# A gated linear attention core rebuilt: wide subtractions, products on VectorE, grouped state updates

## The chip, the cores and the metric

The kernel runs on one core of a Trainium2 chip. The metric is device time in microseconds (us) of one execution, from its launch to its end; lower is better. The median of three runs of the kernel before is 3993.8 us.

## The reference

The program is a backbone of two layers over 2048 latent rows and 256 context rows of 1024 channels, in float32. Layer one is latent attention; the change doesn't touch it. Layer two is bidirectional gated linear attention with 4 heads, 128 key channels and 256 value channels a head. What matters of it, for one direction:

```python
def step(s, inp):
    qc, kc, vc, gc = inp
    bc = jnp.cumsum(gc, axis=2)
    o_inter = jnp.einsum('bhcd,bhde->bhce', qc * jnp.exp(bc), s)
    diff = bc[:, :, :, None, :] - bc[:, :, None, :, :]
    decay = jnp.exp(jnp.where(causal[:, :, None], diff, -jnp.inf))
    a = jnp.einsum('bhid,bhijd->bhij', qc, kc[:, :, None, :, :] * decay)
    o = o_inter + jnp.einsum('bhij,bhje->bhie', a, vc)
    blast = bc[:, :, -1:, :]
    s_new = jnp.exp(blast[:, :, 0, :])[..., None] * s + jnp.einsum('bhcd,bhce->bhde', kc * jnp.exp(blast - bc), vc)
    return s_new, o
```

The outputs of both directions are added, normalised per head, multiplied by silu(gate), projected and added to the stream; a last norm follows.

## The kernel before, in words

Layer two works on chunks of 128 rows, and on blocks of four chunks (512 rows), with channels on the partitions for q, k and the running log decays b. Its input projections are in `fill` (a generator that yields after each small piece: six matmuls of `terms`, L894 to L896, in tile pp). One head's recurrence is in `core(h)`, a generator too.

The loops of a head: first a backward sweep over the context and the blocks 3, 2, 1, 0, which stores the backward state that each chunk reads (s_b); per block `stage1` loads b, k and v, scans the decays (L1026) and makes the decayed keys (`khat`, L1030: subtraction on VectorE, exponential on ScalarE, product on GpSimd), `khat_rows` transposes them (L1045) and copies them to kt_ (L1047), and `update` adds one chunk to the state (L1052, then L1056 on VectorE). Then the blocks 0 to 3 forward. Within a chunk the 128x128 scores are put together by seven levels: at level li the rows are paired in halves of 64 >> li, and each pair of halves meets at the border between them, so that all exponents stay sums of log decays. `factors` (L1091 on) makes one level's decayed q and k in the tile ex (two halves of 512 columns): four subtractions on VectorE (L1102), one exponential on ScalarE (L1103), one product with q and k on GpSimd (L1104). `pairs` multiplies keys by queries in quarters of 64x64 (`quarters`, L1113, tile pg) and puts them into the scores `at`: level 0 as plain copies (L1123, L1124), the others by masked copies (L1128), two per level. `middle` prepares a block (qe, the keys' factors, the diagonal). At the end of a block come the output products (L1197 to L1199, tile po) with a state update after each chunk, the norm, the gate (`gate`, `gate2`: three activations and a product on GpSimd, L1159) and a store.

Factors run two levels ahead of pairs. The order of the work: the program draws pieces of `fill` between the yields of `core`, in proportion to the yields' weights (L1225 on); the framework then sets each engine's order, which may differ a little from the program's:

```python
    NCORE, NFILL, LEAD = 114, 215, 20
    for h in range(3):
        i = 0
        for w in core(h):
            i += w or 1
            while done < NFILL * (h + min(i / NCORE, 1)) + LEAD:
                next(proj, None)
```

With the last head the projections run out; its blocks are then interleaved with the output projection of layer two (`out_all`, tile py).

Of the kernel before, what the change touches and what calls it, by code (L numbers as in the profile page):

```python
# [19 lines left out]
P = 128  # L20
# [4 lines left out]
KT = D // P  # L25
# [10 lines left out]
class K:  # L36
    """Helpers around one TileContext."""
# [17 lines left out]
    def mm3(self, ps, terms):  # L55
        """ps = sum of lhsT.T @ rhs over terms (aH, aL, bH, bL), each product in three exact parts."""
        nc = self.nc
        n = len(terms)
        for i, (ah, al, bh, bl) in enumerate(terms):
            nc.tensor.matmul(ps, ah, bh, start=(i == 0), stop=False)  # L60
            nc.tensor.matmul(ps, ah, bl, start=False, stop=False)  # L61
            nc.tensor.matmul(ps, al, bh, start=False, stop=(i == n - 1))  # L62


def modulation_block(k, layer, nb, w, wp, ps, pt, gT, shT, ng, I, sel, condT, gates, gbc_d, bufs, tag="mod_s", bias=None):
    """512 columns of silu(cond) @ ada_w + ada_b: to shT and gT (channels on the partitions), or as gate rows to DRAM.
    w: the KT row blocks of the weight. Four row blocks at a time, each on its quarter of the array's columns; sel sums."""
# [40 lines left out]
def rstd_col(k, pool, ss, n, mhalf):  # L108
    """(ss / n + eps) ** -0.5 on a column."""
# [8 lines left out]
def body(ctx, tc, I, out, stop=99, dbg=None):  # L118
# [84 lines left out]
    with pool("p1", 2) as sp, pool("ps1", 2, space=PSUM) as psp:  # L203
# [11 lines left out]
        # the columns of shift and scale wait where the gate's weights go later  # L215
# [29 lines left out]
        def kv_weights():  # L245
            """mla_w_ukv in two parts, where the latents' columns were; behind it, the first chunk's kv latents."""
# [174 lines left out]
    def load_k(pr, ci):  # L421
        """One chunk of a pair's keys; what it returns puts it in place, in two parts."""
# [29 lines left out]
    def fetch(limit=2):  # L452
        """The next operands' load, and the parts of those that a former call loaded."""
# [6 lines left out]
    def maxima():  # L460
        """One piece per yield: the maxima of the scores' leading part go to row 96 of the queries."""
# [109 lines left out]
    with pool("p3", 2) as sp, pool("ps3", 2, space=PSUM) as psp:  # L571
# [65 lines left out]
        def mods():  # L637
            """The conditioning that later phases need, in small pieces."""
# [8 lines left out]
        def first_o():  # L647
            """The first rows' attention output, in two parts."""
# [7 lines left out]
        def first_y(oh, ol):  # L656
            """Their output projection, while the last sums are on their way."""
# [11 lines left out]
        def out_load(b):  # L669
            """w_out's rows 512 b and on."""  # L670
# [8 lines left out]
        def out_weights(b, raw):  # L679
            """They go in two parts where the keys were."""  # L680
# [64 lines left out]
    # one head's columns of the GLA input projection, in two parts: [q | gate] (0) or [k | v] (1)  # L745
# [16 lines left out]
    masks = wg.tile([P, 7, P], mybir.dt.uint8, name="masks")  # L762
    reset = wg.tile([P, 512], BF16, name="reset")
    gbias = wg.tile([P, 2, 4], F32, name="gbias")
    def prep_all(sp):
# [3 lines left out]
        for l0, l1 in ((0, 4), (4, 7)):  # L769
            ws = sp.tile([P, 512], F32, name="wsg", tag="wsg", bufs=4)  # L770
            nc.sync.dma_start(ws[:, :P * (l1 - l0)], I["masks"][:, l0:l1, :].rearrange("p l t -> p (l t)"))
            nc.vector.tensor_copy(masks[:, l0:l1, :].rearrange("p l t -> p (l t)"), ws[:, :P * (l1 - l0)])
# [117 lines left out]
    def terms(ps, ts):  # L890
        """ps = the sum over ts, an even share of it per yield."""
# [31 lines left out]
    def keys(h, ci, hk, g):  # L923
        """Columns of q (0) or k (1) of one chunk."""
# [27 lines left out]
    def rows(h, ci, hk, g):  # L952
        """Columns of gate (0) or v (1) of one chunk, rows on the partitions."""
# [14 lines left out]
    def next_h():  # L968
        """The next chunk of h; the one after it is on its way."""
# [6 lines left out]
    def fill():  # L976
        """All projections, a small piece per yield: a head's k, v and decays come with q and gate of the head before."""
# [31 lines left out]

    def block(h, blk, dirs, need_q):  # L1010
# [431 lines left out]
```

## Time and profile before

| what | value |
|---|---|
| runs | 3994.26, 3993.80, 3982.38 us |
| median | 3993.8 us |
| profiled execution, span from first to last instruction | 3977.7 us |
| instructions | 52504 |
| DMA | 451.70 MB, 114 GB/s |

The profile is of one execution; its span is the only time given for it, and it doesn't hold what lies before the first and after the last instruction. PE is TensorE, DVE VectorE, ACT ScalarE, POOL GpSimd. A row of a group of instructions gives line, engine, operation, tiles (written <- read), partitions x elements, count, then busy us and mean ns of one, then the idle time of the engine before them and what ended it. The ends of matmuls are modelled, so a busy PE isn't PE at its peak. TensorE's granted clock is given as a share of 2.4 GHz.

### The profile page before, as it was taken

The page shows a single profiled execution, that of the slowest core. Times are in us where ns is not written, and L with a number is a line of the kernel's source. Part 1 is how long each engine was busy: PE and PEld are TensorE (multiplying, and loading weights), DVE is VectorE, ACT ScalarE, POOL GpSimd, SP SyncE. Part 2 cuts the span into 40 slices and gives each one's busy share as a digit, 9 for nine tenths or more (in the row PEclk, how much of TensorE's full clock was granted, in tenths as well). Part 3 has the DMA queues.
Part 4 walks back from the last instruction along what each step waited for, and adds up shares of the span by engine and source line. Part 5 has one row for each costly group of instructions (what it writes and reads, how often), then busy time and mean ns, then how long its engine had stood idle before and what let it go on. Part 6 is the DMA issues. An engine that isn't in the chain of part 4 may idle for free.

```text
span 3977.7 us, 52504 instructions
## 1 busy us (share of the span) xinstructions
PE 3758.0 (94%) x20446; PEld 2748.3 (69%) x20446; DVE 2527.1 (64%) x3565; ACT 1345.2 (34%) x1879; POOL 1575.1 (40%) x899
## 2 busy tenths in 40 slices
PE   7999999999999999999999999999988889888798
PEld 5777887555555555555555555879977878877577
DVE  4433337777776777777777764652577686776863
ACT  2322222333333333333333433322243333433331
POOL 3121133646354534435363434650344343442430
PEclk9999999999999999999999999999999999999899
DMA  6211564111120201111010101877745546447332
GB/s 219 82 61 45 199 220 142 59 35 49 45 67 34 69 19 57 46 42 49 18 44 15 44 11 62 252 223 247 248 150 188 204 149 224 161 165 249 125 127 96
DMA packets 277393, 451.70 MB, mean 114 GB/s; under 512 B 21892, under 2 KB 178116, under 8 KB 265112
## 3 DMA queue, kind: packets, MB, share of 16 engines
q1 hardware_dynamic: 212648, 371.32, 28.3%
q10 hardware_dynamic: 64496, 77.02, 5.5%
q8 instruction: 161, 2.64, 0.3%
q14 instruction: 88, 0.72, 0.1%
HBM read 307.37 MB, written 140.71 MB: 113 GB/s over the span
## 4 chain that ended last, share of the span: by engine, by line
PE 71%; DVE 12%; issue 7%; DMA 4%; POOL 3%; ACT 1%; SPq 1%; POOLq 0%; ACTq 0%; DVEq 0%
PE st L594 20%; PE po L616 13%; PE pmx L475 8%; DVE ex L1102 5%; PE pj L61 4%; PE pj L60 4%; PE pj L62 4%; PE pp L894 2%; PE pp L896 2%; PE pp L895 2%; POOL ex L1104 1%; PE py L62 1%; PE py L60 1%; PE py L61 1%; DVE at L1128 1%
## 5 line engine op out<-in xcount | busy, mean ns | idle before, releaser
L476 DVE TENSOR_REDUCE mx<-pmx 128x1 f32<-128x512 f32 (+1 forms) x1312 | 762.9, 625 | 317.5 <-PE pmx L475 317.0
L596 ACT ACTIVATE pe<-st 128x1024 f32<-128x1024 f32 (+1 forms) x592 | 599.4, 1013 | 1004.9 <-PE st L594 979.0
L603 POOL TENSOR_TENSOR acc<-acc,pe 128x1024 f32<-128x1024 f32 x192 | 467.9, 2437 | 576.7 <-ACT pe L596 576.3
L616 PE MATMUL po<-pe,vt 128*64 128x512 f32 (+1 forms) x2368 | 572.4, 599 | 0.0
L603 DVE TENSOR_TENSOR acc<-acc,pe 128x1024 f32<-128x1024 f32 x256 | 439.4, 1716 | 96.6 <-ACT pe L596 96.6
L1104 POOL TENSOR_TENSOR ex<-ex,qk 128x1024 f32<-128x1024 f32 x112 | 286.4, 2563 | 285.6 <-ACT ex L1103 279.7
L594 PE MATMUL st<-qs,kb0h 97*128 97x512 f32 (+3 forms) x1184 | 375.4, 396 | 0.1
L594 PE MATMUL st<-qs,kb1h 97*128 97x512 f32 (+3 forms) x1184 | 374.9, 397 | 0.0
L616 PEld LDWEIGHTS po<-pe,vt 128*64 128x64 f32 x2368 | 156.9, 137 | 301.1 <-issue 297.8
L894 PE MATMUL pp<-w,ht 128*128 128x256 f32 x1088 | 334.3, 307 | 0.0
L1102 DVE TENSOR_TENSOR ex<-b 128x256 f32<-128x256 f32 x448 | 300.0, 724 | 16.2 <-PE pg L1113 9.8
L896 PE MATMUL pp<-w,ht 128*128 128x256 f32 x1088 | 309.8, 285 | 0.0
L895 PE MATMUL pp<-w,ht 128*128 128x256 f32 x1088 | 309.6, 285 | 0.0
L594 PEld LDWEIGHTS st<-qs,kb1h 97*128 97x128 f32 (+1 forms) x1184 | 218.3, 190 | 57.9 <-issue 12.2
L594 PEld LDWEIGHTS st<-qs,kb0h 97*128 97x128 f32 (+1 forms) x1184 | 219.9, 191 | 48.9 <-issue 4.2
L594 PE MATMUL st<-qs,kb1l 96*128 96x512 f32 (+1 forms) x592 | 232.3, 392 | 0.0
L594 PE MATMUL st<-qs,kb0l 96*128 96x512 f32 (+1 forms) x592 | 232.3, 392 | 0.0
L894 PE MATMUL pp<-ht,w 128*128 128x256 f32 (+1 forms) x616 | 191.5, 311 | 39.9 <-ACT vge L959 37.9
L1103 ACT ACTIVATE ex<-ex 128x1024 f32<-128x1024 f32 x112 | 118.7, 1060 | 291.7 <-DVE ex L1102 281.8
L475 PE MATMUL pmx<-kb0h,qs 96*128 96x512 f32 (+1 forms) x656 | 208.7, 397 | 8.7 <-DVE mx L476 5.6
L894 PEld LDWEIGHTS pp<-w,ht 128*128 128x128 f32 x1088 | 208.2, 191 | 6.5 <-DVE gm L944 0.2
L895 PEld LDWEIGHTS pp<-w,ht 128*128 128x128 f32 x1088 | 209.4, 192 | 2.5
(393 smaller groups left out, 7487.6 us busy)
## 6 DMA issues: line engine op xcount, KB each, us to landing
ht<-hh_d SPq DMA_DIRECT2D x44, 1024.0 KB
ht<-hl_d SPq DMA_DIRECT2D x44, 1024.0 KB
xt<-in_x SPq DMA_DIRECT2D x32, 512.0 KB
mod_w<-in_ada_w SPq DMA_DIRECT2D x16, 1024.0 KB
v<-gv_d SPq DMA_DIRECT2D x32, 512.0 KB
wsg<-in_gla_w_in SPq DMA_DIRECT2D x66, 192.0 KB
v_d<-vs ACTq DMA_DIRECT2D x18, 512.0 KB
vt<-v_d SPq DMA_DIRECT2D x8, 1152.0 KB
```

The costliest lines, as they stand in the source:

```text
L60: nc.tensor.matmul(ps, ah, bh, start=(i == 0), stop=False)
L475: nc.tensor.matmul(ps[:, :w], qs[0:96, 0, j, t * P:t * P + P], kh[0:96, j, b * 512:b * 512 + w], start=True, stop=True)
L476: nc.vector.reduce_max(mx[:, j * nq + t, b:b + 1], ps[:, :w], axis=AX.X)
L594: nc.tensor.matmul(st[:, j, :n], a, b, start=(i == 0), stop=(i == 2))
L596: nc.scalar.activation(pe[:, :, :n], st[:, :, :n], AF.Exp, scale=SCALE)
L603: eng.tensor_tensor(acc[:, :, :n], acc[:, :, :n], pe[:, :, :n], op=ALU.add)
L616: nc.tensor.matmul(po[64 * j:64 * j + 64, :n], vt[:, kt, 64 * j:64 * j + 64], pe[:, j, :n], start=(kt == 0), stop=(kt == nk - 1))
L894: nc.tensor.matmul(ps, ah, bh, start=(i == 0), stop=False)
L895: nc.tensor.matmul(ps, ah, bl, start=False, stop=False)
L896: nc.tensor.matmul(ps, al, bh, start=False, stop=(i == n - 1))
L1102: nc.vector.tensor_tensor(out_, a_, b_, op=ALU.subtract)
L1104: nc.gpsimd.tensor_tensor(ex, ex, c["qk"], op=ALU.mult)
```

## The change

The four subtractions of a level become one over both directions with all 1024 columns, from the decays at the border to a tile df; two exponentials with scale +1/16 and -1/16 read the right halves of df into ex. The last level, of single rows, decays q alone. The products of q and k (ex), of the state's keys (ke) and of the gate (gt) move from GpSimd to VectorE. The quarters lie side by side in pg (256 columns), and the masked copies go to a compact tile `ad` of 128x256, one per level, which two ScalarE copies place in `at` at the block's end. The state's matmuls of a block are issued together (`updates`), and VectorE's state steps (`advance`) follow. Yields are fewer and carry weights, with a sum of 148 a head. Buffers of df, ke, kt_, at and ad are single. The mask array is 7x64 columns instead of 7x128.

```diff
     def khat(d, qk, b, nch):
...
-        nc.gpsimd.tensor_tensor(e[:, :w], e[:, :w], qk[:, 1, :w], op=ALU.mult)
+        nc.vector.tensor_tensor(e[:, :w], e[:, :w], qk[:, 1, :w], op=ALU.mult)
...
-    def update(khat_c, v_c, tot_c, s_in, s_out):
-        ps = psp.tile([P, 512], F32, name="pk", tag="pk")
-        nc.tensor.matmul(ps[:, :256], khat_c, v_c, start=True, stop=True)
+    def updates(kh, v, chunks):
+        out_ = {}
+        for i, c in enumerate(chunks):
+            if i % 2 == 0:
+                ps = psp.tile([P, 2, 256], F32, name="pk", tag="pk")
+            nc.tensor.matmul(ps[:, i % 2, :], kh[:, c * P:c * P + P], v[:, c, :], start=True, stop=True)
+            out_[c] = ps[:, i % 2, :]
+        return out_
+    def advance(add, tot_c, s_in, s_out):
...
-            nc.vector.scalar_tensor_tensor(s_out, s_in, tot_c, ps[:, :256], op0=ALU.mult, op1=ALU.add)
+            nc.vector.scalar_tensor_tensor(s_out, s_in, tot_c, add, op0=ALU.mult, op1=ALU.add)
...
         def factors(c, li):
...
-            for out_, a_, b_ in ((ev[:, 0, :, 1, :], bv[:, 0, :, 1, :], r0), (ev[:, 0, :, 0, :], bv[:, 1, :, 0, :], r1),
-                                 (ev[:, 1, :, 0, :], r0, bv[:, 0, :, 0, :]), (ev[:, 1, :, 1, :], r1, bv[:, 1, :, 1, :])):
-                nc.vector.tensor_tensor(out_, a_, b_, op=ALU.subtract)
-            nc.scalar.activation(ex, ex, AF.Exp, scale=LOG)
-            nc.gpsimd.tensor_tensor(ex, ex, c["qk"], op=ALU.mult)
-            return ex
+            b = c["b"]
+            if hl == 1:
+                nc.vector.tensor_tensor(view(ex, 0, ((1, 2), (2, 256))), view(b, 512, ((-511, 2), (2, 256))), view(b, 513, ((-513, 2), (2, 256))), op=ALU.subtract)
+                nc.scalar.activation(ex[:, 0, :], ex[:, 0, :], AF.Exp, scale=LOG)
+                nc.vector.tensor_tensor(ex[:, 0, :], ex[:, 0, :], c["qk"][:, 0, :], op=ALU.mult)
+                return ex[:, 0, :], c["qk"][:, 1, :]
+            df = sp.tile([P, 2, 512], F32, name="df", tag="df", bufs=1)
+            nc.vector.tensor_tensor(view(df, 0, ((512, 2), (2 * hl, nn), (1, 2 * hl))), view(b, 0, ((512, 2), (2 * hl, nn), (1, 2 * hl))),
+                                    view(b, hl - 1, ((513, 2), (2 * hl, nn), (0, 2 * hl))), op=ALU.subtract)
+            for i, (o0, s0, sg) in enumerate(((512, hl - 512, LOG), (0, 512 + hl, -LOG))):
+                nc.scalar.activation(view(ex, 512 * i, ((hl, 2), (2 * hl, nn), (1, hl))), view(df, o0, ((s0, 2), (2 * hl, nn), (1, hl))), AF.Exp, scale=sg)
+            nc.vector.tensor_tensor(ex, ex, c["qk"], op=ALU.mult)
+            return ex[:, 0, :], ex[:, 1, :]
...
-            for u in range(2):
-                us = slice(64 * u, 64 * u + 64)
-                nc.vector.copy_predicated(half(c["at"], u, False), masks[us, li, us].unsqueeze(1).to_broadcast([64, 4, 64]), half(pg, u, False))
+            else:
+                nc.vector.copy_predicated(four(c["ad"]), masks[:, li, :].unsqueeze(1).to_broadcast([P, 4, 64]), four(pg))
+        def placed(c):
+            for u in range(2):
+                nc.scalar.copy(half(c["at"], u, False), four(c["ad"], slice(64 * u, 64 * u + 64)))
...
         def gate2(c):
-            sg = sp.tile([P, 4, 256], F32, name="sg", tag="ex", bufs=3)
+            sg = sp.tile([P, 4, 256], F32, name="sg", tag="df", bufs=1)
...
-            nc.gpsimd.tensor_tensor(c["gt"], c["gt"], sg, op=ALU.mult)
+            nc.vector.tensor_tensor(c["gt"], c["gt"], sg, op=ALU.mult)
...
                 pairs(c, li, exs[li])
-                yield 2
+                if li % 2 == 0:
+                    yield 5 if li in (2, 4) else 3
             c["kh"] = khat_rows(c["ke"], 4)
+            placed(c)
...
+            add = updates(c["kh"], c["v"], [i for i in range(4) if 4 * blk + i < 15])
+            ss = [s]
+            for i in range(4):
+                if i in add:
+                    s2 = sp.tile([P, 256], F32, name="sf", tag="sf", bufs=5)
+                    advance(add[i], c["tot"][:, 0, i:i + 1], ss[i], s2)
+                    ss.append(s2)
+            s = ss[-1]
+            yield 8 if cn else 2
...
-    NCORE, NFILL, LEAD = 114, 215, 20
+    NCORE, NFILL, LEAD = 148, 215, 20
...
-        while done < NFILL * 3 + LEAD + i * 1.2:
+        while done < NFILL * 3 + LEAD + i * 0.92:
...
-    for _ in main:
-        for _ in range(4):
+    for w in main:
+        for _ in range(round(2 * w)):
```

## Rows read from the trace of the kernel before

**Rows 1.** The page's first part: busy us (share of the span) x instructions.

```profile
PE 3758.0 (94%) x20446; PEld 2748.3 (69%) x20446; DVE 2527.1 (64%) x3565; ACT 1345.2 (34%) x1879; POOL 1575.1 (40%) x899
```

**Rows 2.** Busy time by stretch: length, busy us of each engine, TensorE's clock, DMA.

```profile
core 0: us, PE busy (x) PEld busy (x) DVE busy (x) ACT busy (x) POOL busy (x), PEclk, DMA share, GB/s
2820.00:3084.00 264.00, 230.07 (x2004) 215.47 (x2003) 189.11 (x298) 96.41 (x176) 111.92 (x62) 0.95 0.55 185
3084.00:3342.00 258.00, 223.31 (x1941) 207.75 (x1940) 189.23 (x299) 97.05 (x177) 109.41 (x62) 0.95 0.53 182
3342.00:3602.00 260.00, 227.49 (x1961) 210.74 (x1960) 185.88 (x294) 98.24 (x180) 104.55 (x54) 0.95 0.56 188
3602.00:3710.00 108.00, 79.39 (x626) 69.60 (x624) 82.75 (x121) 37.10 (x69) 37.81 (x18) 0.87 0.63 220
3710.00:3786.00 76.00, 61.49 (x349) 47.22 (x350) 59.08 (x89) 27.63 (x45) 29.74 (x15) 0.87 0.33 110
3786.00:3978.00 192.00, 177.80 (x967) 139.91 (x965) 96.07 (x161) 50.40 (x87) 38.38 (x27) 0.98 0.32 110
```

**Rows 3.** What TensorE waited for, 2850 to 3870: us in total, times, longest.

```profile
PE pg L1113 <- POOL ex L1104: 43.8, 34, 7.0
PE pp L894 <- ACT vge L959: 37.3, 9, 8.2
...
PE pk L1052 <- ACT kt__29738 L1047: 5.4, 1, 5.4
```

**Rows 4.** Who waited for whom, all engines, 2850 to 3870.

```profile
ACT ex L1103 <- DVE ex L1102: 281.8, 92, 7.3
POOL ex L1104 <- ACT ex L1103: 279.7, 90, 9.7
```

**Rows 5.** The timeline of two levels in head two: start us, us, engine, what.

```profile
3149.37 2.38 POOL L1104 TENSOR_TENSOR ex<-ex,qk 128x1024 f32<-128x1024 f32 x1 [3.91 <-ACT ex L1103]
...
3149.62 3.43 DVE L1102 TENSOR_TENSOR ex<-b 128x256 f32<-128x256 f32 x4
...
3153.14 1.06 ACT L1103 ACTIVATE ex<-ex 128x1024 f32<-128x1024 f32 x1 [3.85 <-DVE ex L1102]
...
3154.05 3.60 DVE L1102 TENSOR_TENSOR ex<-b 128x256 f32<-128x256 f32 x4
...
3154.28 2.42 POOL L1104 TENSOR_TENSOR ex<-ex,qk 128x1024 f32<-128x1024 f32 x1 [2.53 <-ACT ex L1103]
```

**Rows 6.** Durations of single lines: ns min/median/max, first and last start.

```profile
L1102 DVE TENSOR_TENSOR ex<-b x448: 402/418/2622, 2855.1 to 3866.0; 128x256 f32<-128x256 f32 x150
...
L1139 DVE TENSOR_TENSOR qe<-qe,qk x16: 1207/1227/2571, 2858.2 to 3780.1; 128x1024 f32<-128x1024 f32 x16
...
L1036 DVE TENSOR_TENSOR ke<-b x37: 418/680/2819, 2828.4 to 3740.2; 128x512 f32<-128x512 f32 x30, 128x256 f32<-128x256 f32 x7
...
L1037 ACT ACTIVATE ke<-ke x37: 408/632/640, 2829.1 to 3740.9; 128x512 f32<-128x512 f32 x30, 128x256 f32<-128x256 f32 x7
...
L1026 DVE TENSOR_TENSOR_SCAN b<-reset,b x53: 684/1225/3380, 2826.9 to 3739.1; 128x512 f32<-128x512 bf16 x46, 128x256 f32<-128x256 bf16 x7
```

**Rows 7.** VectorE's costliest groups in head two, 3084 to 3342.

```profile
L1102 DVE TENSOR_TENSOR ex<-b 128x256 f32<-128x256 f32 x112 | 75.9, 732 | 4.1 <-PE pg L1113 3.5
L1026 DVE TENSOR_TENSOR_SCAN b<-reset,b 128x512 f32<-128x512 bf16 (+1 forms) x14 | 22.2, 1594 | 8.8 <-DMA b<-ggf_d 4.7 <-DMA b<-ggb_d 4.1
L1128 DVE COPY_PREDICATED at<-masks,pg 64x256 f32<-64x256 uint8 x48 | 21.5, 448 | 2.5 <-PE pg L1113 1.2
```

**Rows 8.** VectorE's timeline in head two, 3133 to 3144.

```profile
3133.31 0.41 DVE L1054 COPY sf<-pk 128x256 f32<-128x256 f32 x1
...
3141.97 0.45 DVE L1128 COPY_PREDICATED at<-masks,pg 64x256 f32<-64x256 uint8 x1 [0.62 <-PE pg L1113]
3142.31 0.73 DVE L944 TENSOR_SCALAR gm<-pp,gbias 128x512 f32<-128x512 f32 x1
3143.08 0.46 DVE L1128 COPY_PREDICATED at<-masks,pg 64x256 f32<-64x256 uint8 x1
```

**Rows 9.** What VectorE waited for in head two, 3084 to 3342.

```profile
DVE s_b L1056 <- PE pk L1052: 11.7, 8, 2.6
DVE sf L1056 <- PE pk L1052: 10.8, 7, 2.5
```

More of the change, by code (lines that the diff above doesn't have):

```diff
@@ L768, in prep_all @@
             yield
[L769 to L772, printed above, removed]
+        ws = sp.tile([P, 512], F32, name="wsg", tag="wsg", bufs=4)
+        nc.sync.dma_start(ws[:, :7 * 64], I["masks"].rearrange("p l t -> p (l t)"))
+        nc.vector.tensor_copy(masks.rearrange("p l t -> p (l t)"), ws[:, :7 * 64])
         nc.vector.memset(reset, 1.0)
@@ L1008, in body, with view @@
     psp = cst.enter_context(pool("psc", 2, space=PSUM))
+    def view(t, off, dims):
+        a = t[:, 0, 0:1]
+        return bass.AP(tensor=a.tensor, offset=a.offset + off, ap=[list(a.ap[0])] + [list(d) for d in dims])
     def block(h, blk, dirs, need_q):
@@ L1072, in core @@
             kh = khat_rows(e, nch)
-            yield
+            yield 1
             if bi + 1 < len(order):
                 nxt = stage1(order[bi + 1])
-                yield
-            for i in range(nch - 1, -1, -1):
-                kc, vc, tc_ = kh[:, i * P:i * P + P], v[:, i, :], tot[:, 1, i:i + 1]
+                yield 2
+            chunks = [i for i in range(nch - 1, -1, -1) if blk < 0 or 4 * blk + i > 0]
+            add = updates(kh, v, chunks)
+            for i in chunks:
                 if blk < 0:
-                    update(kc, vc, tc_, None if i == 1 else sc, sc if i == 1 else s_b[:, 15, :])
-                elif 4 * blk + i > 0:
+                    advance(add[i], tot[:, 1, i:i + 1], None if i == 1 else sc, sc if i == 1 else s_b[:, 15, :])
+                else:
                     n = 4 * blk + i
-                    update(kc, vc, tc_, s_b[:, n, :], s_b[:, n - 1, :])
-                yield
-        s = None
-        qk, b, v, tot, nch = block(h, -1, (0,), False)
-        kh = khat_rows(khat(0, qk, b, nch), nch)
-        yield
+                    advance(add[i], tot[:, 1, i:i + 1], s_b[:, n, :], s_b[:, n - 1, :])
+            yield nch / 2
         def factors(c, li):
@@ L1158, in gate2 @@
             nc.scalar.activation(sg, sg, AF.Exp, scale=-1.0)
-            nc.gpsimd.tensor_tensor(c["gt"], c["gt"], sg, op=ALU.mult)
+            nc.vector.tensor_tensor(c["gt"], c["gt"], sg, op=ALU.mult)
+        qk, b, v, tot, nch = block(h, -1, (0,), False)
+        kh = khat_rows(khat(0, qk, b, nch), nch)
+        yield 1
         c = begin(0)
-        yield
+        yield 2
+        add = updates(kh, v, (0, 1))
+        s = None
         for i in range(2):
-            s2 = sp.tile([P, 256], F32, name="sf", tag="sf")
-            update(kh[:, i * P:i * P + P], v[:, i, :], tot[:, 0, i:i + 1], s, s2)
+            s2 = sp.tile([P, 256], F32, name="sf", tag="sf", bufs=5)
+            advance(add[i], tot[:, 0, i:i + 1], s, s2)
             s = s2
-            yield
+        yield 1
         middle(c)
         exs = [factors(c, 0), factors(c, 1)]
-        yield
+        yield 6
         for blk in range(4):
```

76 lines of the change are left out of this document (35 added, 41 removed).

## The prediction

> **What bounds the kernel now.** The page's first part comes first: TensorE is busy 3758.0 of 3977.7 us [rows 1]. That is an average over stages, so the stages follow. From 2820 us on the recurrence of layer two is woven into its projections. The stretches of the first three heads (264, 258 and 260 us, cut where a head's last block leaves) show TensorE busy 230.07, 223.31 and 227.49 us at a granted clock of 0.95, the start of the fourth head 79.39 of 108 us and 61.49 of 76 us at 0.87 [rows 2]. Idle time in these five is 33.9 + 34.7 + 32.5 + 28.6 + 14.5 = 144 us. A clock of 0.95 is a tenth of the time at 1.2 GHz instead of 2.4 GHz, after stretches in which TensorE waited; a tenth of 258 us at half speed is worth up to 13 us a head. So a head has at most 34.7 + 13 = 48 us to give, and its TensorE work is about 210 us. The last stretch, from 3786 us on, is busy 177.80 of 192 us [rows 2]: there TensorE is the bound.
>
> What it waits for stands in the waits: 43.8 us for the product ex on GpSimd (L1104), 37.3 us for the ScalarE copy vge that empties a projection's PSUM bank, and waits of up to 5.4 us for kt_, ScalarE's copy of the transposed keys [rows 3]; the kt_ wait occurs nine times, 25.6 us together. Behind these is a chain: ScalarE's exponential waits 281.8 us for VectorE's subtractions, GpSimd's product 279.7 us for that exponential [rows 4]. vge stands behind those exponentials on ScalarE. The timeline of two levels shows why the chain is slow [rows 5]: at 3149.62 VectorE starts four subtractions and ends them after 3.43 us, while GpSimd's product of the level before runs from 3149.37 for 2.38 us; at 3154.05 the same again, 3.60 us. A level takes 3154.05 - 3149.62 = 4.4 us there, and 4.9 us from product to product; I take 4.5. One subtraction alone takes 0.402 to 0.418 us, but the slowest 2.622, about a product longer [rows 6], and the mean in head two is 0.732 [rows 7]. So the two engines take turns, and the level costs their sum.
>
> **The change part by part, for one block of 512 rows.** A head is four blocks and a backward sweep. Head two (3084 to 3342) spends some 49 us on the sweep, up to the first sf copy at 3133.31 [rows 8], and 209 on four blocks: 52.3 each; TensorE's share of the 48 us is some 8.5 a block, the most a block can win.
>
> *Subtraction and product.* Four subtractions become one of 1024 elements. Nearest row: qe (L1139), a 128x1024 operation of two SBUF operands, one broadcast, 1.227 us median [rows 6]. The product on VectorE has the same shape: 1.227. The masked copy goes from two of 64x256 (mean 0.448 [rows 7]) to one of 128x256; same columns, 0.45. VectorE's work in a wide level is then 1.23 + 1.23 + 0.45 = 2.9 us, and the last level has half the elements: 0.68 + 0.68 + 0.45 = 1.8, with 0.68 from ke (L1036, 512 elements [rows 6]).
>
> *The new wait.* The product now stands on VectorE behind the subtraction and needs the exponentials between: two of 512 elements, 0.632 each by ke's exponential (L1037 [rows 6]), 1.26 us. The buffer df is single, so the next subtraction can't go ahead of them either. Whatever is queued behind the product (masked copies, state advances, VectorE's copies out of projection banks) waits too. Bounds of a wide level: 2.9 if all of this is filled, 2.9 + 1.26 = 4.15 if none. I take the middle, 3.5: the order on VectorE isn't the program's, a projection's gm stands between two masked copies of one level [rows 8], so part of the gap will be filled, but VectorE's ready work there is thin. Levels of a block: before 7 x 4.5 = 31.5; after 6 x 3.5 + 1.8 + 0.6 = 23.4. **Gain 8.1.** Bounds: 6 x 2.9 + 1.8 = 19.2 gives 12.3, 6 x 4.15 + 2.4 = 27.3 gives 4.2.
>
> *Work that comes to VectorE besides.* The keys' product (0.68) and the gate's product (1.23) leave GpSimd, with waits behind one exponential (0.63) and behind three of 1.06 us [rows 5]. Surely 1.9 us a block, at worst 1.9 + 0.63 + 3.2 = 5.7. Scans lose their turns with GpSimd: 1.594 mean against 1.225 median [rows 6, 7], two a block, 0.7 back. I take 2.5 net, nearer the low end, as the gate's loads and exponentials come two levels ahead of its use. **Net gain 8.1 - 2.5 = 5.6 a block**, under the 8.5. Twelve blocks of three heads: **67 us**.
>
> *State updates in groups.* VectorE waits in head two 11.7 and 10.8 us for single updates from TensorE [rows 9]; TensorE waits for kt_ as above. With all update matmuls together, more projection pieces stand between the transposes and the first update (3 x 215/148 = 4.4 instead of 2 x 215/114 = 3.8 in the sweep), and output matmuls no longer alternate with VectorE's state. Ends: nothing, and the 25.6 us of kt_. Two thirds of that lies in forward blocks, where the cap already counts it. I take **8 us**.
>
> *Fourth head.* From 3602 to 3786 projections run out and TensorE idles 43 us [rows 2], so the block's chain shows in full: two blocks x 5.6, and its kt_ wait of 5.4 [rows 3]: **17 us**. Its last two blocks lie under the output projection; nothing, since TensorE covers them; without that cover they would cost or give 5.6 each.
>
> *At nothing.* The masks' load and conversion become one each, before the first head, under projections. Fewer buffers (ke, kt_, at): each waits for transposes or products that precede it in program order; at worst 37 keys x the 1 us of a short wait, hidden while VectorE has other work. One exponential more per level, one scaling less and two placing copies more a block on ScalarE: about 2 us a block on an engine busy under half the time. New weights at the yields (148 for 114) keep 215 pieces of projection a head; a block gets 31 x 215/148 = 45 instead of 36, the sweep fewer. The levels keep 16/31 of a block's pieces instead of 14/19, which follows the shorter levels. On GpSimd the weight splits and the power of orr are freed of the queue.
>
> Sum: 67 + 8 + 17 = 92 us. The page gives the profiled execution's span, 3977.7 us, 16.1 under the median of the three runs, which also holds what lies around the span; nothing around it changes. 3993.8 - 92 = **3902 us**.
>
> **Rivals.** *VectorE becomes the bound.* For it: in head two its busy time barely falls. 112 subtractions (75.9 us) and 48 masked copies (21.5) go [rows 7]; 24 x 1.23 + 4 x 0.68 = 32 come for subtractions, 32 for products, 11 for masked copies, 6 for keys, 5 for the gate: 189 [rows 2] becomes 178, less 5 for scans. If every wait is exposed a block gains 4.2 - 5.0 = -0.8. Against it: order is free [rows 8]. Twelve blocks lose 10, the state groups give 8: about 3995 us. The Trainium skill, page "TensorE: Matmul & The Clock Gate", section Part 1, says of the architecture that VectorE's queue is strictly first in, first out. By that rule a product whose exponential is late holds all that was queued behind it, and the time would be this rival's unless the order was chosen well beforehand; the trace agrees in that VectorE sat idle for single updates [rows 9]. Chance 0.11.
>
> *The strided exponential is dear, and the kernel gets slower.* No row shows ScalarE reading and writing runs of 2 to 64 elements. If such an exponential costs twice the contiguous one, 1.26 us, a wide level is 2.9 + 2.5 = 5.4 us, 0.9 over today: 6 x 0.9 + 2.5 = 8 us a block lost, 14 blocks, 112 us: 4106. It decides from (4.5 - 2.9)/2 = 0.8 us each with nothing filled in. Against it: VectorE's subtractions have the same runs and stay at 0.418 [rows 6]. Chance 0.09.
>
> *The waits vanish.* TensorE is kept fed: 12 x 8.5 + 15 + 40 = 157 us: 3837. For it: 2.9 us a level. Chance 0.12. The forecast, from a quarter to all of the waits filled short of that, has 0.68.
>
> **The numbers.** The range 3835 to 3970 holds the forecast's bounds and the floor; it leaves out the slow rival and most of the first. 0.3% is 12 us, about what a measurement of this kernel can tell. Faster: 0.68 + 0.12 + half of 0.11; same: the rest of that; slower: 0.09.
>
> **What would show it.** Right: the wide subtraction and the product near 1.23 us; ScalarE's strided exponentials near 0.63; levels 3.5 us apart; TensorE's idle time in a head under 20 us and the clock near 1; GpSimd a few us a head. Wrong: blocks still 52 us apart with VectorE waiting for ex from ScalarE; exponentials over 0.8 us; the idle time moved to pp after vge, because ScalarE's copies now stand behind exponentials that wait for a later subtraction; po waiting for at behind the placing copies.

## The result and the profile after

| | before | after |
|---|---|---|
| median of 4 runs each, in turn on one chip | 3989.18 us (3982.38 to 3994.26) | 3832.68 us (3830.01 to 3834.88) |
| ratio, 95% interval | | 0.9623 [0.9597, 0.9648] |
| span of the profiled execution | 3977.7 us | 3828.1 us |

The kernel is 156 us faster, 150 in the profiled spans. The forecast was 92 us. The measured median lies 2.3 us under the low end of its range; the kernel before came out 4.6 us lower in this timing than the 3993.8 that the forecast starts from, and the ratio gives 0.9623 x 3993.8 = 3843 us, inside the range near that end. The time is about that of the rival "the waits vanish" (3837). The whole page first, as [rows 1]: GpSimd lost 380 us of busy time, VectorE 121, TensorE 55 at the same number of matmuls.

```profile
PE 3702.5 (97%) x20446; PEld 2717.6 (71%) x20446; DVE 2406.3 (63%) x3300; ACT 1356.5 (35%) x1991; POOL 1194.7 (31%) x731
```

The same six stretches as [rows 2], cut where a head's last block or the fourth head's first two leave (columns as there):

```profile
2820.00:3055.00 235.00, 224.38 (x2032) 213.46 (x2031) 157.84 (x229) 99.73 (x206) 13.85 (x20) 0.97 0.62 208
3055.00:3274.00 219.00, 210.35 (x1952) 199.17 (x1951) 160.01 (x236) 99.43 (x205) 13.91 (x20) 1.00 0.65 215
3274.00:3490.00 216.00, 209.48 (x1945) 198.23 (x1944) 160.03 (x232) 102.50 (x211) 8.40 (x12) 1.00 0.70 235
3490.00:3578.00 88.00, 69.79 (x605) 63.90 (x603) 71.87 (x99) 39.09 (x77) 1.85 (x1) 0.92 0.73 258
3578.00:3641.00 63.00, 56.95 (x348) 45.35 (x350) 48.61 (x66) 25.95 (x51) 2.67 (x4) 0.89 0.37 126
3641.00:3828.00 187.00, 176.12 (x986) 140.40 (x980) 89.52 (x134) 52.51 (x99) 9.81 (x15) 0.99 0.32 113
```

The stretches got 29, 39, 44, 20, 13 and 5 us shorter: 150, so the whole gain lies here. In head two TensorE's idle time went from 34.7 to 8.65 us, which is 26 of its 39; the other 13 are busy time (223.31 to 210.35 for 1941 and 1952 matmuls), with the granted clock up from 0.95 to 1.00. Over the first three heads the idle time fell by 75 us (101.1 to 25.8), the busy time by 37; over the fourth by 22 and 16.

Head two once more, cut between its backward sweep and its blocks, before and then after (columns as in [rows 2]):

```profile
3084.00:3133.00 49.00, 45.32 (x349) 43.78 (x348) 28.33 (x49) 17.30 (x33) 14.84 (x9) 1.00 0.74 257
3133.00:3342.00 209.00, 178.00 (x1594) 163.97 (x1593) 160.90 (x252) 79.75 (x144) 94.56 (x54) 0.94 0.49 164
```

```profile
3055.00:3093.00 38.00, 36.09 (x268) 33.94 (x266) 29.69 (x48) 15.79 (x33) 0.00 (x0) 1.00 0.87 295
3093.00:3274.00 181.00, 174.27 (x1686) 165.23 (x1685) 130.33 (x189) 83.64 (x172) 13.91 (x20) 1.00 0.60 198
```

Before, the sweep was nearly full (TensorE idle 3.7 of 49 us) and the blocks were not (31 of 209). After, some 80 to 90 matmuls have moved from the sweep into the blocks, and the blocks are shorter all the same. In every head, from the single records (a sweep runs from the end of the head before, in head one from 2820, to VectorE's first copy sf; the blocks from there to VectorE's last scaling of osb):

| head | sweep before | after | blocks before | after |
|---|---|---|---|---|
| one | 50.7 | 34.7 | 213.3 | 200.7 |
| two | 49.3 | 37.5 | 209.1 | 181.1 |
| three | 52.3 | 38.6 | 207.3 | 177.9 |
| four | 45.4 | 32.4 | 266.0 | 240.4 |

Of the 112 us of heads one to three, 42 lie in the sweeps and 70 in the twelve blocks; of the fourth head's 38, 13 lie in its sweep.

What TensorE waited for (2850 to 3720), beside [rows 3]:

```profile
PE pg L1131 <- DVE at L1141: 12.2, 2, 10.5
PE pp L893 <- ACT vge L958: 9.4, 6, 4.0
PE pg L1131 <- DVE ex L1118: 8.3, 5, 3.7
```

And the two waits of a level's chain, from the waits of all engines, beside [rows 4]:

```profile
ACT ex L1117 <- DVE df L1114: 132.9, 64, 6.2
...
DVE ex L1118 <- ACT ex L1117: 28.1, 41, 1.4
```

The wait for the product ex fell from 43.8 us to 8.3, that for vge from 37.3 to 9.4. VectorE stood still before its product for 28.1 us in all: 96 wide levels with two exponentials of 0.631 us each could have cost 121. How it is filled shows in VectorE's and ScalarE's timeline of two levels in head two:

```profile
3105.93 1.21 DVE L1114 TENSOR_TENSOR df<-b 128x1024 f32<-128x1024 f32 x1
3107.06 1.00 DVE L1143 COPY_PREDICATED ad<-masks,pg 128x256 f32<-128x256 uint8 x2
3107.25 1.15 ACT L1117 ACTIVATE ex<-df 128x512 f32<-128x512 f32 x2 [4.88 <-DVE df L1114]
3108.44 1.23 DVE L1118 TENSOR_TENSOR ex<-ex,qk 128x1024 f32<-128x1024 f32 x1 [0.38 <-ACT ex L1117]
3109.58 1.22 DVE L1114 TENSOR_TENSOR df<-b 128x1024 f32<-128x1024 f32 x1
...
3112.14 1.23 DVE L1118 TENSOR_TENSOR ex<-ex,qk 128x1024 f32<-128x1024 f32 x1 [1.34 <-ACT ex L1117]
```

Two masked copies of earlier levels stand in the first gap; the second level finds nothing and waits 1.34 us. From the start of the subtraction to the end of the product the first level takes 3109.67 - 3105.93 = 3.74 us. Before, it took 3156.70 - 3149.62 = 7.08 [rows 5].

VectorE's groups in head two beside [rows 7], and ScalarE's exponential there:

```profile
L1114 DVE TENSOR_TENSOR df<-b 128x1024 f32<-128x1024 f32 x24 | 29.4, 1227 | 0.0
L1118 DVE TENSOR_TENSOR ex<-ex,qk 128x1024 f32<-128x1024 f32 x24 | 29.2, 1219 | 5.7 <-ACT ex L1117 5.5
L1030 DVE TENSOR_TENSOR_SCAN b<-reset,b 128x512 f32<-128x512 bf16 (+1 forms) x14 | 16.0, 1142 | 3.6 <-DMA b<-ggb_d 3.6
L1143 DVE COPY_PREDICATED ad<-masks,pg 128x256 f32<-128x256 uint8 x24 | 10.7, 447 | 1.0 <-PE pg L1131 0.4
...
L1117 ACT ACTIVATE ex<-df 128x512 f32<-128x512 f32 x48 | 28.6, 631 | 35.4 <-DVE df L1114 35.4
```

**Delay, not pace.** From the single records of head two I took, for each level, the time from the start of its first subtraction to the end of its product:

| kernel | product on | levels | shortest / median / longest, us |
|---|---|---|---|
| before | GpSimd | 28 | 5.04 / 7.24 / 13.32 |
| after | VectorE | 24 wide | 3.66 / 4.26 / 16.57 |
| before, product moved (below) | VectorE | 28 | 3.78 / 5.38 / 11.19 |
| after, narrow subtractions (below) | VectorE | 28 | 3.78 / 4.92 / 9.47 |
| after, product moved back (below) | GpSimd | 24 wide | 5.00 / 7.18 / 21.73 |

The distance between levels changed far less. A block has two runs of wide levels, the first three ahead of the output products of the block before and the next three behind them. The gaps from one product's start to the next inside these runs, 48 in heads one to three, have a median of 4.6 us before and 4.3 after, a mean of 4.6 and 4.5. What became shorter in a block is the stretch between its two runs, from the third level's product to the fourth's (19.2 to 13.4 us, mean of 12), and from its last level to the next block's first (10.2 to 8.7, mean of 9).

### The profile page after: what moved, and what is told of

It reads as the page before. It is cut to its first block, busy times and chain, and to the rows that moved or that the text cites. A ratio compares the mean times of both kernels' runs of the same rounds, so it can differ in the third digit from the quotient of the medians.

```text
span 3828.1 us, 51918 instructions
## 1 busy us (share of the span) xinstructions
PE 3702.5 (97%) x20446; PEld 2717.6 (71%) x20446; DVE 2406.3 (63%) x3300; ACT 1356.5 (35%) x1991; POOL 1194.7 (31%) x731
## 4 chain that ended last, share of the span: by engine, by line
PE 76%; DMA 7%; DVE 6%; issue 6%; POOL 3%; ACT 2%; SPq 1%; POOLq 0%; ACTq 0%; DVEq 0%
PE st L594 20%; PE po L616 14%; PE pmx L475 8%; PE pj L61 5%; PE pj L60 5%; PE pj L62 5%; PE pp L893 2%; PE pp L894 2%; PE pp L895 2%; DMA wsg<-in_gla_w_in 2%; PE py L893 1%; PE py L895 1%; PE py L894 1%; PE pk L1060 1%; PE py L62 1%
## 5 line engine op out<-in xcount | busy, mean ns | idle before, releaser
L893 PE MATMUL pp<-w,ht 128*128 128x256 f32 x1088 | 317.9, 292 | 0.0
L894 PE MATMUL pp<-w,ht 128*128 128x256 f32 x1088 | 305.9, 281 | 0.0
L895 PE MATMUL pp<-w,ht 128*128 128x256 f32 x1088 | 304.9, 280 | 0.0
L1242 POOL TENSOR_TENSOR orr<-oss,mhalf 128x4 f32<-128x4 f32 x16 | 17.1, 1068 | 659.3 <-DVE oss L1241 659.3
L475 PE MATMUL pmx<-kb1h,qs 96*128 96x512 f32 (+1 forms) x656 | 205.0, 396 | 4.1 <-DVE mx L476 4.0
L893 PEld LDWEIGHTS pp<-w,ht 128*128 128x128 f32 x1088 | 205.8, 189 | 3.4
L894 PEld LDWEIGHTS pp<-w,ht 128*128 128x128 f32 x1088 | 205.9, 189 | 1.1
L895 PEld LDWEIGHTS pp<-w,ht 128*128 128x128 f32 x1088 | 205.5, 189 | 0.1
L475 PEld LDWEIGHTS pmx<-kb1h,qs 96*128 96x128 f32 x656 | 114.0, 189 | 120.9 <-issue 73.7
```

Source lines behind the costliest of these rows:

```text
L475: nc.tensor.matmul(ps[:, :w], qs[0:96, 0, j, t * P:t * P + P], kh[0:96, j, b * 512:b * 512 + w], start=True, stop=True)
```

## The experiments

Each ratio is to the kernel before, timed in turn with it; 0.001 is 4 us. "Over after" is the ratio less 0.9623, times 3985 us; the two intervals together leave about 11 to 14 us either way. Theories: (A) GpSimd's product was the late step, and its move is the main gain; (B) the wide subtraction, or (C) the new dealing of the work, is. (The recorded texts call (B) what the run in hand sets against (A).)

### The product back on GpSimd

```diff
-            nc.vector.tensor_tensor(ex, ex, c["qk"], op=ALU.mult)
+            nc.gpsimd.tensor_tensor(ex, ex, c["qk"], op=ALU.mult)
```

The last level's product goes with it.

> The changed kernel with the products of q and k (ex) back on GpSimd, all else as changed. Theory A (the two engines taking turns, and the chain through GpSimd, were the cost): 50 to 90 us over the changed kernel's 3833, so 3883 to 3923; the wide subtraction's mean rises from 1.23 us to over 1.8, TensorE's idle time in a head rises by 15 us or more, again before pg after ex. Theory B (grouped updates and new weights made the gain; the engine of the product matters little): under 15 us over 3833, although subtractions stretch.

Measured: 3905.97 us, 0.9802 [0.9778, 0.9826], 71 us over after. VectorE's subtraction and GpSimd's product in head two, then TensorE's wait for it (2850 to 3800):

```profile
L1114 DVE TENSOR_TENSOR df<-b 128x1024 f32<-128x1024 f32 x24 | 51.8, 2160 | 3.2 <-ACT ex L1117 3.1
```

```profile
L1118 POOL TENSOR_TENSOR ex<-ex,qk 128x1024 f32<-128x1024 f32 x24 | 65.6, 2740 | 77.8 <-ACT ex L1117 34.9 <-PE pp L894 33.2 <-issue 7.2
```

```profile
PE pg L1131 <- POOL ex L1118: 23.4, 10, 4.5
```

The wide subtraction grows from 1.227 to 2.160 us, and the product takes 2.740 instead of 1.219: the turns of [rows 5, 6] are back, and TensorE waits for the product again. The time and the durations are those that (A) expected; TensorE's idle time in head two rises by 9 us, not by 15.

### The product alone, in the kernel before

The kernel before with the one line of the diff above, the other way round (L1104).

> The kernel before with one edit: the products ex move to VectorE. If the move is the main part by itself: 60 to 90 us under the kernel before (3985), as putting it back cost 73. If it needs the rest (the wide subtraction, the compact copies, the new weights) to be worth anything: under 30 us.

Measured: 3884.73 us, 0.9742 [0.9725, 0.976], 103 us under before. Head two, and TensorE's wait for the product (2850 to 3870):

```profile
3051.00:3286.00 235.00, 218.65 (x1944) 205.09 (x1944) 180.56 (x328) 97.39 (x177) 39.58 (x34) 0.98 0.60 201
```

```profile
PE pg L1113 <- DVE ex L1104: 28.5, 18, 5.4
```

One word of the program gives 103 of the 150 us. VectorE's busy time in the head falls, 189.23 [rows 2] to 180.56, though it took over 28 products of 1.219 us: its 112 narrow subtractions went from a mean of 0.732 [rows 7] to 0.475. It is more than the 60 to 90 us expected. By the same cuts as above, the blocks of heads two and three take 185.4 and 180.7 us here, about as in the changed kernel, but the sweeps 49.6 and 49.2, as before: of the 55 us by which the changed kernel's span is still shorter, 48 lie in the four sweeps.

### Narrow subtractions

```diff
-            nc.vector.tensor_tensor(view(df, 0, ...), view(b, 0, ...), view(b, hl - 1, ...), op=ALU.subtract)
+            for out_, a_, b_ in (...):
+                nc.vector.tensor_tensor(out_, a_, b_, op=ALU.subtract)
+            nc.scalar.activation(ex, ex, AF.Exp, scale=LOG)
```

The changed kernel with the four subtractions and the one exponential of before; the product stays on VectorE.

> The changed kernel with the four narrow subtractions and the one exponential of before, the product on VectorE. Theory A: VectorE works 4 x 0.42 - 1.23 = 0.45 us more a level, 50 us in all, most of it under TensorE: 5 to 20 us over 3833. Rival (VectorE's own work sets the pace of a level, so that the wide subtraction is the main part of the gain): 40 us or more over 3833, blocks 3 us longer.

Measured: 3837.76 us, 0.9626 [0.9601, 0.965], 1 us over after. With the product on VectorE, (B) falls, and even the 5 to 20 us of (A) are not seen: without GpSimd's product beside them the four take 4 x 0.428 us (a mean over 112 in head two), against 1.227 for one wide, and the half microsecond a level is not seen.

### Narrow subtractions and the product on GpSimd

Both edits together: of the change only the rest is left (dealing of the work, compact masked copies, keys' and gate's products on VectorE, grouped updates).

> The changed kernel with both halves of a level as before (four narrow subtractions, one exponential, product on GpSimd). What is left against the kernel before is the grouping, the weights, the compact masked copies and the keys' and gate's products on VectorE. If all of the gain lies in the levels' subtraction and product: about the kernel before, over 3950. If the rest has a part of its own of about half: 3890 to 3930.

Measured: 3929.47 us, 0.9855 [0.9835, 0.9874], 58 us under before. So the rest alone gives 58, the product alone 103, both with the wide subtraction 150: an overlap of 11 us, no more than the intervals leave open. Against the product back on GpSimd with the wide subtraction kept (0.9802), the narrow ones cost 21 us, by some 12 either way: beside GpSimd's product the wide subtraction is worth something, without it 1 us. TensorE's wait for the product even grew, from 43.8 us to (2850 to 3800)

```profile
PE pg L1126 <- POOL ex L1113: 69.4, 29, 8.4
```

### Work on GpSimd that nobody waits for

```diff
+            nc.scalar.copy(tok, df[:, 0, 0:1])
+            for i in range(3):
+                nc.gpsimd.tensor_tensor(scr, c["qk"][:, i // 2, ...], tok.to_broadcast([P, 256]), op=ALU.mult)
             nc.vector.tensor_tensor(ex, ex, c["qk"], op=ALU.mult)
```

Each wide level of the changed kernel gives GpSimd products whose result is not used, so that the turns stay and the dependence does not. To make room, both forms also put the tile sc among the buffers of sf. A first form used two products of 512 columns and a single buffer for the small copy:

> The changed kernel with two GpSimd operations of 512 elements a level that nobody waits for (some 2.4 us a level, as the product took; one tiny ScalarE copy sets them going). It adds the turns without the chain. If the turns themselves are the cost: VectorE's wide operations stretch by 0.3 us or more in the mean and the time rises by 20 to 60 us. If the chain through GpSimd (waiting for its result) was the cost: under 12 us over 3833, whatever VectorE's durations do.

Measured: 3961.53 us, 0.9937 [0.9913, 0.9961], 125 over after. It settles nothing: with one buffer ScalarE's next small copy waited for GpSimd, and what stood behind it on ScalarE with it (2850 to 3720):

```profile
ACT tok L1120 <- POOL scr L1122: 157.4, 68, 3.8
```

The second form, as in the diff, has 16 buffers for it:

> As the run before with GpSimd work that nobody waits for, but set going by a one-element ScalarE copy into one of sixteen small tiles, so that ScalarE never waits for GpSimd (there it did: one tile served for all, and the copies held ScalarE's queue). Three GpSimd operations of 256 elements a level, some 2.2 us. Turns alone as the cost: 30 us or more over the changed kernel's 3833, wide operations of VectorE over 1.5 us in the mean. The chain through GpSimd's result as the cost: under 15 us.

Measured: 3857.07 us, 0.9674 [0.9658, 0.9691], 20 over after, with 3 x 1.037 us of GpSimd a level. VectorE's subtraction and product in head two:

```profile
L1116 DVE TENSOR_TENSOR df<-b 128x1024 f32<-128x1024 f32 x24 | 33.9, 1414 | 0.0
L1126 DVE TENSOR_TENSOR ex<-ex,qk 128x1024 f32<-128x1024 f32 x24 | 30.4, 1268 | 6.2 <-ACT ex L1119 6.1
```

That is between what was expected of the two causes, 30 or more and under 15. The turns cost some 20 us here, by some 12 either way, and they were milder (1.414 us a subtraction against 2.160 with the real product). So a part of the 71 us is turns; how the other 50 divide between longer turns and waiting for the slow product stays open.

### VectorE in the program's order

```diff
-    nc.vector.<any operation of layer two>(...)
+    tc.keep_in_program_order(nc.vector.<the same>(...))
```

The same instructions; the framework no longer chooses VectorE's order.

> The changed kernel with every VectorE instruction of layer two kept in the program's order, so that the product stands right behind its subtraction in 84 of 96 wide levels and VectorE waits for both exponentials. If filling that wait is what made the gain larger than the prediction's middle: 40 us or more over 3833, VectorE waiting over 80 us for ex. If TensorE has slack enough for it: under 15 us.

Measured: 4009.02 us, 1.0058 [1.004, 1.0077]: 173 over after, and slower than before. All VectorE operations go through one line here (L889). Waits of all engines from 2850 to 3870, then of TensorE:

```profile
DVE ex L889 <- ACT ex L1134: 107.4, 83, 3.9
```

```profile
PE pg L1148 <- DVE at L889: 43.2, 13, 21.2
PE pg L1148 <- DVE ad L889: 39.8, 21, 5.0
PE pg L1148 <- DVE ex L889: 35.5, 14, 4.8
```

In this order the product stands directly behind its subtraction in 84 of 96 wide levels, in the changed kernel in 11. VectorE's wait for the exponentials grows from 28.1 to 107.4 us, near the 121 that nothing filled would give, and the masked copies behind it (ad) come late for TensorE. The edit fixes the order of everything on VectorE, not of the product alone, so 173 is the price of all of it. Up to the end of head three the span is 72 us longer than the changed kernel's; the larger part, some 108, comes behind it, where projections run out and TensorE idles 113 of 445 us at a clock of 0.85 (in the changed kernel 35 of 338):

```profile
3563.00:4008.00 445.00, 332.27 (x1925) 267.77 (x1923) 221.59 (x308) 123.88 (x235) 12.72 (x20) 0.85 0.34 118
```

### Single state updates

```diff
-            add = updates(c["kh"], c["v"], [i for i in range(4) if 4 * blk + i < 15])
...
+                    if n < 15:
+                        s2 = sp.tile([P, 256], F32, name="sf", tag="sf", bufs=5)
+                        advance(updates(c["kh"], c["v"], [i])[i], c["tot"][:, 0, i:i + 1], s, s2)
```

One update behind each chunk's output product, and one yield after each, as before; in the sweep too, updates come one at a time. The sum of the weights is kept.

> The changed kernel with one state update at a time, each followed by a yield, the sums of the weights kept. Theory A with the prediction's term for the groups: 5 to 15 us over 3833, with TensorE again waiting for kt_ and VectorE for single updates. Theory B: 40 us or more, since the groups would be a main part of the gain.

Measured: 3839.72 us, 0.9631 [0.9607, 0.9655], 3 over after. No effect that can be told from none, and none of the 40 us of the second theory, although VectorE's wait of sf for pk comes back in part (head two, 3066 to 3284):

```profile
DVE sf L1068 <- PE pk L1060: 8.5, 5, 2.9
...
DVE osb L1231 <- PE po L1225: 7.4, 3, 2.9
```

Against 0.3 us in the changed kernel; but there VectorE's wait of osb for po is 16.4. The wait moved.

### Keys' and gate's products back on GpSimd

```diff
-        nc.vector.tensor_tensor(e[:, :w], e[:, :w], qk[:, 1, :w], op=ALU.mult)
+        nc.gpsimd.tensor_tensor(e[:, :w], e[:, :w], qk[:, 1, :w], op=ALU.mult)
...
-            nc.vector.tensor_tensor(c["gt"], c["gt"], sg, op=ALU.mult)
+            nc.gpsimd.tensor_tensor(c["gt"], c["gt"], sg, op=ALU.mult)
```

> The changed kernel with two of its moves undone: the product for the state's keys (37 of them) and the product for the gate (16) go back to GpSimd; the product of the levels stays on VectorE. Everything before showed the levels' product to carry about 100 us; of the other 56 us that the rest of the change gave, these two moves may be a part. If VectorE's time decides, as the prediction's term of 2.5 us a block has it, undoing gives time back: 10 to 30 us faster than the changed kernel, about 3805 to 3823. If GpSimd's slower product and the taking of turns are what cost, it is slower: 16 x 1.2 + 37 x 0.55 = 40 us of longer products at most, some 15 of them seen, 3840 to 3870. If neither engine is near the path, within 8 us of 3833.

Measured: 3853.31 us, 0.9674 [0.966, 0.9688], 20 over after. Head two: the subtraction now waits for the gate's product, since both use the buffer df, and GpSimd needs 2.374 us for it. That wait belongs to the single buffer of df: in the kernel before, the gate's tile sg was one of the three buffers of ex.

```profile
L1114 DVE TENSOR_TENSOR df<-b 128x1024 f32<-128x1024 f32 x24 | 31.0, 1292 | 2.6 <-POOL gt L1177 2.6
```

```profile
L1177 POOL TENSOR_TENSOR gt<-gt,sg 128x1024 f32<-128x1024 f32 x4 | 9.5, 2374 | 51.8 <-ACT sg L1176 51.8
```

### Masked copies in place

```diff
-                nc.vector.copy_predicated(four(c["ad"]), masks[:, li, :]..., four(pg))
+                for u in range(2):
+                    us = slice(64 * u, 64 * u + 64)
+                    nc.vector.copy_predicated(half(c["at"], u, False), masks[us, li, :]..., four(pg, us))
```

The diagonal goes in place too, and the two placing copies go.

> The changed kernel without the compact tile: two masked copies of 64x256 a level straight into the scores, no placing copies on ScalarE at the block's end. VectorE gets 96 masked copies more, 96 x 0.45 = 43 us in all. If VectorE's time decides the blocks, some 38 us of it show: 3870. If VectorE has room (73% busy in head two) and TensorE is kept fed, at most 10 us: 3833 to 3843. If the placing copies at the block's end hold the output products up (four waits of po for the scores), it may even be faster, by up to 5 us.

Measured: 3845.9 us, 0.9659 [0.9643, 0.9675], 14 over after. VectorE's busy time in head two rises by 12 us (160.01 to 172.45), of which 24 more copies of 0.447 make 11; the head gets 4 us longer, so two thirds are covered. The 14 us lie between the two expectations, and just outside what the intervals leave open.

```profile
3055.00:3278.00 223.00, 212.87 (x1942) 200.72 (x1941) 172.45 (x256) 99.07 (x201) 14.63 (x20) 0.98 0.63 211
```

### The old shares of projection pieces

```diff
-                if li % 2 == 0:
-                    yield 5 if li in (2, 4) else 3
+                yield (23 if blk < 3 else 18) / 7
...
-            yield 8 if cn else 2
+            yield 4.5 if cn else 1.5
```

With 0.5 for 2 after the next block's loads, 0.75 for 1.5 between output products, 1.5 for 2 at the end.

> The changed kernel with the block's pieces of projection dealt out as in the kernel before: 23 of a block's 31 parts after the seven levels one by one, the rest thin (0.5 behind the next block's loads, 4.5 ahead of the output products, 0.75 between them), same sum. If the new weights are a part of the 56 us that the rest of the change gave, it is slower by 15 us or more, 3848 to 3880, with TensorE idle at the block's ends, where updates and output products stand close together. If the levels' speed alone matters, within 8 us of 3833.

Measured: 3848.97 us, 0.9665 [0.9651, 0.968], 17 over after. Head two, and the two of its 12 us stretches in which the clock was lowest:

```profile
3046.00:3274.00 228.00, 219.31 (x1954) 205.88 (x1953) 159.28 (x233) 100.17 (x207) 15.45 (x20) 0.98 0.62 207
```

```profile
3058.00:3070.00 12.00, 9.69 (x61) 9.08 (x61) 7.60 (x14) 5.09 (x10) 0.00 (x0) 0.86 0.71 230
...
3166.00:3178.00 12.00, 11.66 (x80) 10.92 (x81) 8.97 (x12) 8.34 (x17) 0.00 (x0) 0.73 0.55 197
```

A stretch of the changed kernel with as much idle time as the one ahead of the second of these:

```profile
3199.00:3211.00 12.00, 9.39 (x123) 8.89 (x122) 8.43 (x13) 4.94 (x6) 3.07 (x5) 1.00 0.62 181
```

The time is what was expected, but not the reason: TensorE's idle time in the head is that of the changed kernel, 8.7 us; the 9 us more are busy time at a clock of 0.98 instead of 1.00. At 0.73 TensorE had just been idle for 2.8 of the 12 us before (busy 9.23). In the changed kernel it idled 2.6 of the 12 us from 3199, and the clock was 1.00 there and behind it. Why the same idle time costs the clock in one kernel and not in the other is not shown. The sweep keeps its share of the pieces in this run and stays short, 38.8 us.

### Pieces kept for the fourth head

```diff
-    NCORE, NFILL, LEAD = 148, 215, 20
+    NCORE, NFILL, LEAD = 148, 215, 4
...
-        while done < NFILL * 3 + LEAD + i * 0.92:
+        while done < NFILL * 3 + LEAD + i * 1.1:
```

> The changed kernel with 16 pieces of projection kept back for the fourth head (the lead falls from 20 to 4, and the fourth head draws 1.1 pieces for a weight of 1 instead of 0.92). TensorE idles 18 us in the first 88 us of the fourth head at a clock of 0.92, and 16 pieces are some 14 us of TensorE. If that idle time is for want of projections, 5 to 14 us faster: 3819 to 3828. If it is a chain of waits that no piece fits into, or if heads one to three become short of pieces, no change or slower by up to 10.

Measured: 3826.11 us, 0.9612 [0.959, 0.9633]: 4 us under after, within the interval and short of the 5 to 14 expected. In the fourth head's first stretch TensorE's idle time falls from 18.2 to 13.6 us, in the second it rises from 6.1 to 10.5; the want of pieces moved on by one block.

```profile
3482.00:3568.00 86.00, 72.45 (x621) 65.66 (x619) 69.21 (x94) 38.85 (x78) 0.65 (x1) 0.94 0.76 272
3568.00:3633.00 65.00, 54.47 (x328) 43.46 (x329) 51.16 (x68) 27.10 (x52) 2.65 (x5) 0.87 0.35 117
```

## Why the prediction was right, and where it was not

**What bounds the kernel: right.** A head had "at most 34.7 + 13 = 48 us to give", idle time and clock. Head two gave 26 and 13. That the product on GpSimd was the step TensorE waited for is shown by moving that product alone, 103 us one way and 71 the other; that VectorE and GpSimd took turns, by the subtractions, which the move took from 0.732 to 0.475 us one way and from 1.227 to 2.160 the other.

**The durations: right.** Subtraction and product were put at 1.227 us and took 1.227 and 1.219; the exponential of 0.632 took 0.631, the masked copy of 0.45 took 0.447, the scan's mean fell from 1.594 to 1.142 (1.219 for those of 512 columns, where 1.225 was expected). The rival with the dear strided exponential falls on the exponential's row.

**Where the 58 us lie.** The change gave 150 us in the span, 58 more than forecast. By place: the twelve blocks 70 for the 67 forecast; the sweeps of heads one to three 42, where of the 8 us of the state groups a part had been counted and nothing else; the fourth head 38 for 17, of which 13 are its sweep.

**The weights "at nothing": the term that failed.** The prediction saw that "a block gets 31 x 215/148 = 45 instead of 36" pieces of projection, "the sweep fewer", and priced this at nothing. The sweep's loop had 27 of the 114 parts of a head's yields and has 22 of 148, 51 and 32 of 215 pieces; in head two its matmuls fell from 349 to 268, and it became 12 us shorter. TensorE was nearly full in the sweep and idle for 31 us in the blocks, so pieces that move from the one to the other shorten the sweep and cost the blocks little once their levels come in time. That the weights do this, and not another part of the change, is argued from what else was undone: with single updates the sweep of head two takes 37.4 us, with the keys' product on GpSimd 38.0, with the old shares inside the blocks 38.8, with masked copies in place 37.2; with the old weights and the product moved it takes 49.6. No run gave the sweep its old pieces back by itself. The old shares inside a block cost another 17 us.

**The pace of a level: wrong, though the blocks' sum came out.** The prediction took 4.5 us a level before and "the middle, 3.5" after, and made the block's gain of 8.1 us from it. The middle meant that half of the 1.26 us of exponentials is exposed, (3.5 - 2.9) / 1.26 = 48%; in head two it was 5.5 of 24 x 1.26 = 30 us, 18%. But the levels did not come 3.5 us apart: 4.3 in the median, against 4.6. Blocks still shrank, in head two from 52.3 to 45.3 us (from VectorE's first sf copy at 3092.91 to 3274), 7.0 each, over the first three heads 5.8 each, where 5.6 was forecast, and that with more pieces in them. So 67 against 70 is luck in part: the gain lies between the runs of levels and not in them. What shortened besides is the delay from a subtraction to the end of its product, 7.24 to 4.26 us. My reading is that TensorE has projection pieces between the levels and only waits when a level is late. It is not shown: no run changed the delay and the pace apart from each other, and with narrow subtractions the delay is 4.92 us and the time that of the changed kernel.

**The net of 2.5 us for the keys' and gate's products: wrong in sign.** It was counted as a loss of 12 x 2.5 = 30 us on VectorE. Undoing it costs 20 us (0.9674 against 0.9623), by some 12 either way. How this divides between the longer products, the turns and the wait for the shared buffer is not shown.

**State updates in groups, 8 us: not resolved**, 3 us with an uncertainty of some 14. The longest kt_ wait did go down, from 5.4 us [rows 3] to 1.0 (2850 to 3720).

**The fourth head, 17 us: mis-sized.** It gave 20 + 13 + 5 = 38, of which 13 are its sweep, which the term of two blocks and a kt_ wait left out. That projections run out there was right: TensorE still idles 24 us in its first two stretches at a clock of 0.92 and 0.89.

**The rivals.** "VectorE becomes the bound" had 3995 us and a chance of 0.11. The changed kernel isn't there, but in the program's order the same instructions give 4009. The Trainium skill, page "TensorE: Matmul & The Clock Gate", section Part 1, calls VectorE's queue strictly first in, first out; the traces agree: in that order VectorE stood 107.4 us for exponentials and held the masked copies behind it. What keeps the rival away is the order chosen beforehand, which puts other work between subtraction and product. "The waits vanish", 0.12, came in its total and in TensorE being fed: 157 us worked out there, 150 in the span, and idle time of 50 us in the five stretches that had 144. But it put 12 x 8.5 = 102 us on the blocks, which gave 70, and left at most 15 for the sweeps of heads one to three, which gave 42. Its chance was too low for want of the pieces that changed place; the exposed wait, where a row (a projection's gm between two masked copies, [rows 8]) spoke for the lower end, was priced too high as well.

## What to carry to other kernels

Moving the last step of a chain to an engine that is twice as fast for it, and that had been slowed by the sharing, gave two thirds of this gain with one word. Where an engine that bounds has other work to draw on, look at how late a side chain's result comes, and not only at how often; that is a reading of these records, not a result. Price where filler work stands as well: pieces taken out of a stretch that was full and put into one that had idle time went with sweeps 54 us shorter over four heads here, a gain that the forecast had at nothing; by elimination, as said above, the weights did it. When a step is moved onto a busy in-order engine, look at what order its queue gets: the same instructions were 4% faster than before or 0.6% slower. A loss that is priced from an engine's busy time alone (keys, gate) can have the wrong sign when the engine has room and the place left was the slower one.

## What was not expected of the hardware

An exponential over runs of 64 down to 2 columns costs ScalarE no more than a contiguous one: 0.612 to 0.703 us over 192 of 512 columns, median 0.631, against 0.632 [rows 6]. A masked copy from PSUM over 128 partitions takes 0.447 us, the same as one over 64 (0.448 [rows 7]), so two half copies cost twice one whole. And the price of GpSimd's products to VectorE is large on operations with two inputs in SBUF, but not on that masked copy: with the product back on GpSimd the wide subtraction went from a mean of 1.227 to 2.160 us, the keys' product (eight of 512 columns and two of 256 in head two) from a mean of 0.634 to 1.065, the masked copy stayed (0.444).
